# Feed-forward input products by one level of Strassen's scheme, gated features through DRAM, output projection as a stage of its own

## The chip, the core and the metric

The kernel runs on one core of a Trainium2 chip. The metric is device time in microseconds (us); the lower the better. Before the change three runs gave 3990.24, 3992.53 and 3998.9 us, median 3992.53.

## The reference, cut to what matters

Two trunk layers, each with a mixer and then a SwiGLU feed-forward block. There are 1152 tokens (128 of context, 1024 latent), the model width is 1024, the hidden width 2816. All data are float32. The change touches the feed-forward block of both layers alone:

```python
def swiglu(h, w_in, w_out):
    g, u = jnp.split(h @ w_in, 2, axis=-1)
    return (jax.nn.silu(g) * u) @ w_out
...
lat = lat + m_lat[5] * swiglu(modulate(rms_norm(lat, norm_ffn_g[layer]), m_lat[3], m_lat[4]), w_ffn_in[layer], w_ffn_out[layer])
```

## The kernel before

Activations are kept feature-major: 8 tiles of 128 features by 1152 tokens. Every float32 operand of a large product is split into a high part in the matmul's reduced float32 format (fp32r) and a low part, the rest; `mm3` (L79) then forms a product by three matmuls, high·high, high·low and low·high, into one PSUM bank. `hH`, `hL` are the two parts of the normed input, `wh`, `wl` those of a weight.

The feed-forward block (`ffn`, L1655) goes through 22 blocks `f` of 128 hidden features. For each it loads the gate and the up weights (8 DMAs of 128 KB), splits them (ScalarE copies to the high part at L73, VectorE subtracts at L74), and forms, for each of three groups of 384 tokens, the gate product and the up product: 3 x 2 x 8 x 3 = 144 matmuls of 384 columns. ScalarE applies silu (L1689), VectorE multiplies by the up product (L1690), ScalarE and GpSimd split the result into `gh`, `gl` (L1691, L1692). After each second `f` the output projection of the pair follows (`out_tg`, L760): 3 token groups x 8 output blocks x 6 matmuls, and VectorE adds the result to the residual `x` (L769). So a layer issues 22 x 144 = 3168 input matmuls and 1584 output matmuls, all of 384 columns.

Two other streams run beside it. At the block's start the norm of the last token group (`norm_fm`, L340) is still under way; `tail_step` advances it during `f` = 0. In layer 0 the modulation vector of layer 1 is formed on VectorE (`ada_vec`, L203: 96 steps, each a 256 KB load `aw` and two instructions over 512 elements at L221 or L223; the sums over partitions are 192 one-column matmuls, L229); `ffn` takes one or two steps after each token group.

The order on each engine's queue is set when the kernel is built, by a scheduler that follows the program's order and buffer releases; on the chip each queue runs in that order, except that semaphores make it wait. The lines around the change:

```python
hid.append((gh, gl))
if len(hid) == 2:
    ws = [self.out_w(wo, f - 1 + i, p) for i in range(2)]
    out = self.out_steps(l, 5, x, *zip(*hid), *zip(*ws), ps, post)
...
for _ in itertools.islice(side, 2 if (f + tg) % 2 else 1):
    pass
```

Of the kernel before, what the change touches and what calls it, by code (L numbers as in the profile page):

```python
# [20 lines left out]
P = 128  # L21
# [22 lines left out]
class Net:  # L44
# [25 lines left out]
    def split(self, hi, lo, src, scale=None):  # L70
        nc = self.nc
        if scale is None:
            nc.scalar.copy(hi, src)  # L73
            nc.vector.tensor_tensor(lo, src, hi, op=ALU.subtract)  # L74
        else:
            nc.scalar.mul(hi, src, scale)
            nc.vector.scalar_tensor_tensor(lo, src, scale, hi, op0=ALU.mult, op1=ALU.subtract)
# [1574 lines left out]
        return np_, hp, hH, hL  # L1652


    def ffn(self, l, x, hH, hL, p, ps, last, side):  # L1655
# [3 lines left out]
        hid = []  # L1659
        for f in range(NF):  # L1660
            WH, WL = [], []
            for kb in range(4):
                raw = self.t(p, [P, 2, 2, P], tag="wraw")
                for u in range(2):
                    nc.sync.dma_start(raw[:, :, u, :], wi[:, kb * 2 : kb * 2 + 2, u, f * P : (f + 1) * P])
                wh = self.t(p, [P, 2, 2, P], F32R, tag="wh")
                wl = self.t(p, [P, 2, 2, P], F32R, tag="wl")
                self.split(wh, wl, raw)
                WH.append(wh)
                WL.append(wl)  # L1670
# [3 lines left out]
            post = last() if f == NF - 1 else None  # L1674
            if len(hid) == 2:
                ws = [self.out_w(wo, f - 1 + i, p) for i in range(2)]
                out = self.out_steps(l, 5, x, *zip(*hid), *zip(*ws), ps, post)
            for tg in range(TG):
                sl = slice(tg * GW, (tg + 1) * GW)
                pg = []  # L1680
                for u in range(2):
                    pt = self.t(ps, [P, 512], tag="mm")
                    for k in range(KT):
                        self.mm3(pt[:, :GW], WH[k // 2][:, k % 2, u, :], WL[k // 2][:, k % 2, u, :], hH[k][:, sl], hL[k][:, sl], k == 0, k == KT - 1)
                    pg.append(pt)
                    if f == 0:
                        self.tail_step()
                s = self.t(p, [P, GW], tag="fs", bufs=2)
                nc.scalar.activation(s, pg[0][:, :GW], AF.Silu)  # L1689
                nc.vector.tensor_tensor(s, s, pg[1][:, :GW], op=ALU.mult)  # L1690
                nc.scalar.copy(gh[:, sl], s)  # L1691
                nc.gpsimd.tensor_tensor(gl[:, sl], s, gh[:, sl], op=ALU.subtract)  # L1692
                for _ in itertools.islice(side, 2 if (f + tg) % 2 else 1):
                    pass
                if post is not None:
                    for _ in range(KT):
                        next(out)
            if len(hid) == 2:
                for _ in out:
                    pass  # L1700
                hid = []


    def norm_out(self, x, gb, p, tg):
# [163 lines left out]
    def ffn_block(self, l, x, hp, hH, hL, np_):  # L1868

        nc = self.nc  # L1870
        with ExitStack() as es:
            p = _Bufs(es.enter_context(self.pool(f"ff{l}", "right" if l else "left")), {"wraw": 3, "wh": 6, "wl": 6, "gh": 3, "gl": 3, "owraw": 1, "owh": 2, "owl": 2, "aw": 2})
            ps = _Bufs(es.enter_context(self.pool(f"psf{l}", space=PSUM)), {"mm": 8})

            self.nps = ps

            def spill_norm(tg):
                sl = slice(tg * GW, (tg + 1) * GW)
                for k in range(KT):
                    nc.sync.dma_start(self.xsp[k, :, sl], x[k][:, sl])  # L1880
                yield from self.norm_fm(1, 1, 0, x, hH, hL, np_, tg)

            def last():
                if l == 0:
                    self.xsp = self.dram.tile([KT, P, TOK], F32, name="xsp")
                    return spill_norm
                np_.release()
                p2 = es.enter_context(self.pool("fin", "right"))
# [163 lines left out]
```

## Time and profile before

| | |
|---|---|
| runs | 3990.24, 3992.53, 3998.9 us |
| profiled execution | 3991.86 us, span 3990.1 us |
| mean granted TensorE clock | 0.973 of full speed |
| TensorE matmul busy | 3790.7 us of the span |
| VectorE, ScalarE, GpSimd busy | 2169.5, 1250.4, 711.9 us |
| feed-forward block, layer 0 | from 960.72 us to 1819.9 us |
| feed-forward block, layer 1 | from 3130.11 us to 3975.2 us |

PE is TensorE's matmul, PEld its weight load, DVE is VectorE, ACT ScalarE, POOL GpSimd, SP the queue that issues most DMAs. A duration is that of one instruction as the profiler saw it; matmuls overlap, so the time that one costs in a stream is the distance from start to start. PEclk is the granted clock.

### The profile page before, as it was taken

The numbers are of one execution on the slowest core, as the hardware profiler recorded it, in microseconds if no ns is written. First come the engines' busy times: TensorE is split into PE (matmuls) and PEld (weight loads), VectorE is DVE, ScalarE is ACT, GpSimd is POOL, SyncE is SP. The second block draws the span as 40 slices with busy tenths as digits, with TensorE's granted clock in tenths as the row PEclk, the third lists the DMA queues.
The fourth block names the chain that finished last, engine by engine and source line by source line (L and its number), as shares of the span: only waits on it lengthen the run. The fifth ranks groups of instructions, "written<-read, shape, count | busy, mean of one in ns | idle before, by whom it ended". The sixth has DMA issues, their size and how long they took to land.

```text
span 3990.1 us, 62872 instructions
## 1 busy us (share of the span) xinstructions
PE 3790.7 (95%) x23989; PEld 3559.6 (89%) x23989; DVE 2169.5 (54%) x5159; ACT 1250.4 (31%) x2930; POOL 711.9 (18%) x730
## 2 busy tenths in 40 slices
PE   8999997999999999998999998888888999999998
PEld 5899997999999999998989876776777999999998
DVE  5666665666454545345254656888875543343343
ACT  4555545555111111115232322233222411111112
POOL 3321202202100000012011232233322300000000
PEclk9999998999999999999999997999999999999999
DMA  6533316432222222213243434222223211111111
GB/s 203 150 105 91 95 52 163 126 85 88 67 80 64 85 64 80 69 46 116 87 129 102 163 123 142 66 70 63 64 64 103 64 38 45 41 37 43 43 40 53
DMA packets 378086, 339.98 MB, mean 85 GB/s; under 512 B 65428, under 2 KB 328720, under 8 KB 376248
## 3 DMA queue, kind: packets, MB, share of 16 engines
q1 hardware_dynamic: 359344, 324.37, 27.0%
q10 hardware_dynamic: 13160, 7.27, 0.7%
q0 software_dynamic: 5280, 4.31, 0.5%
q8 instruction: 190, 3.11, 0.3%
q14 instruction: 112, 0.92, 0.1%
HBM read 263.37 MB, written 72.38 MB: 84 GB/s over the span
## 4 chain that ended last, share of the span: by engine, by line
PE 78%; DVE 10%; DMA 5%; issue 3%; ACT 2%; POOL 1%; SPq 0%; ACTq 0%; DVEq 0%; POOLq 0%
PE mm L81 17%; PE mm L83 17%; PE mm L82 17%; PE o L522 3%; PE mm L390 2%; PE mm L392 2%; PE mm L391 2%; PE T L516 1%; DVE MB L1241 1%; DVE tf L1240 1%; PE mm L857 1%; PE A L1190 1%; PE mm L859 1%; PE mm L858 1%; PE S L558 1%
## 5 line engine op out<-in xcount | busy, mean ns | idle before, releaser
L81 PE MATMUL mm<-hH,wh 128*128 128x384 f32 x2544 | 865.1, 341 | 20.2 <-DVE nv L363 12.6
L82 PE MATMUL mm<-hL,wh 128*128 128x384 f32 x2544 | 860.6, 339 | 2.5 <-DVE hL L366 2.5
L83 PE MATMUL mm<-hH,wl 128*128 128x384 f32 x2544 | 859.8, 339 | 0.0
L769 DVE SCALAR_TENSOR_TENSOR x<-mm,mod,x 128x384 f32<-128x384 f32 (+2 forms) x896 | 431.5, 512 | 197.5 <-PE mm L83 195.8
L81 PEld LDWEIGHTS mm<-hH,wh 128*128 128x128 f32 x2544 | 480.0, 189 | 31.4 <-ACT wh L73 18.8
L82 PEld LDWEIGHTS mm<-hL,wh 128*128 128x128 f32 x2544 | 480.1, 189 | 5.6 <-DVE hL L366 2.7
L83 PEld LDWEIGHTS mm<-hH,wl 128*128 128x128 f32 x2544 | 480.0, 189 | 4.0 <-issue 2.9
L1692 POOL TENSOR_TENSOR gl<-fs,gh 128x384 fp32r<-128x384 f32 x132 | 140.4, 1063 | 1484.1 <-ACT gh L1691 1484.1
L74 DVE TENSOR_TENSOR wl<-wraw,wh 128x512 fp32r<-128x512 f32 (+2 forms) x360 | 217.9, 618 | 336.0 <-ACT wh L73 306.4
L82 PE MATMUL mm<-gl,owh 128*128 128x384 f32 x1056 | 353.0, 334 | 0.0
L83 PE MATMUL mm<-gh,owl 128*128 128x384 f32 x1056 | 352.9, 334 | 0.0
L81 PE MATMUL mm<-gh,owh 128*128 128x384 f32 x1056 | 350.4, 335 | 0.0
L1690 DVE TENSOR_TENSOR fs<-fs,mm 128x384 f32<-128x384 f32 x132 | 73.0, 553 | 430.3 <-PE mm L83 424.7
L73 ACT CAST wh<-wraw 128x512 fp32r<-128x512 f32 (+2 forms) x360 | 188.2, 530 | 205.5 <-DMA wraw<-in_w_ffn_in_dram 77.3
L73 ACT CAST owh<-owraw 128x1024 fp32r<-128x1024 f32 x60 | 62.9, 1049 | 489.7 <-PE mm L82 446.0
L390 PE MATMUL mm<-wh,hH 128*128 128x384 f32 x576 | 199.3, 346 | 3.8 <-ACT ist L408 3.7
L82 PEld LDWEIGHTS mm<-gl,owh 128*128 128x128 f32 x1056 | 198.3, 188 | 0.1
L83 PEld LDWEIGHTS mm<-gh,owl 128*128 128x128 f32 x1056 | 198.2, 188 | 0.0
L81 PEld LDWEIGHTS mm<-gh,owh 128*128 128x128 f32 x1056 | 197.8, 188 | 0.3 <-DVE x L769 0.3
L391 PE MATMUL mm<-wl,hH 128*128 128x384 f32 x576 | 195.3, 339 | 0.0
L392 PE MATMUL mm<-wh,hL 128*128 128x384 f32 x576 | 194.0, 338 | 0.0
L1689 ACT ACTIVATE fs<-mm 128x384 f32<-128x384 f32 x132 | 64.9, 492 | 383.5 <-PE mm L83 383.4
(385 smaller groups left out, 7437.8 us busy)
## 6 DMA issues: line engine op xcount, KB each, us to landing
wraw<-in_w_ffn_in_dram SPq DMA_DIRECT2D x352, 128.0 KB
aw<-in_w_ada_dram SPq DMA_DIRECT2D x160, 256.0 KB
owraw<-in_w_ffn_out_dram SPq DMA_DIRECT2D x44, 512.0 KB
F<-stg SPq DMA_DIRECT2D x34, 640.0 KB
stg<-st SPq DMA_DIRECT2D x12, 1536.0 KB
qkv<-ist SPq DMA_DIRECT2D x72, 192.0 KB
wraw<-in_w_in_attn_dram SPq DMA_DIRECT2D x64, 192.0 KB
nab<-rpbd SPq DMA_DIRECT2D x64, 192.0 KB
```

What stands on the lines that cost most here:

```text
L73: nc.scalar.copy(hi, src)
L74: nc.vector.tensor_tensor(lo, src, hi, op=ALU.subtract)
L81: mm(out, lhsT=wh, rhs=xh, start=first, stop=False)
L82: mm(out, lhsT=wh, rhs=xl, start=False, stop=False)
L83: mm(out, lhsT=wl, rhs=xh, start=False, stop=last)
L390: mm(pt[:, :ncol], lhsT=hH[k][:, c], rhs=WH[k], start=k == 0, stop=False)
L391: mm(pt[:, :ncol], lhsT=hH[k][:, c], rhs=WL[k], start=False, stop=False)
L392: mm(pt[:, :ncol], lhsT=hL[k][:, c], rhs=WH[k], start=False, stop=k == KT - 1)
L522: nc.tensor.matmul(o, lhsT=pT[:, i * P : (i + 1) * P], rhs=vs(b + i), start=b + i == 0, stop=b + i == nk - 1)
L769: self.nc.vector.scalar_tensor_tensor(x[f][:, c], pt[:, a:b], self.mod[l][jg][:, f, cd : cd + 1], x[f][:, c], op0=ALU.mult, op1=ALU.add)
L1690: nc.vector.tensor_tensor(s, s, pg[1][:, :GW], op=ALU.mult)
L1692: nc.gpsimd.tensor_tensor(gl[:, sl], s, gh[:, sl], op=ALU.subtract)
```

## The change

The input products of `f` = 1 to 21 use one level of Strassen's scheme in Winograd's form. The 2x2 blocks of the weights are (gate, up) by two halves of the 1024 input features, those of the activations the two halves of the features by two halves of the tokens (576 each). Seven block products take the place of eight: each has 2 column chunks of 288 x 4 feature tiles x 3 matmuls, so 168 matmuls of 288 columns for one `f`. `f` = 0 stays as it was.

The scheme needs combined operands. `forms` makes them from `hH` and `hL` at the start of each block: T1, T2, T3 in new tiles and a fourth in place of `hH[0:4]`, `hL[0:4]` in the second token half, in chunks of 192 and 384 columns, on VectorE, GpSimd and ScalarE; T2 is first read by the third product of `f` = 1, T3 by the fifth, the fourth form by the sixth. `prep` combines and splits the weights of each `f` (7 splits, 4 VectorE and 3 GpSimd subtractions of 512 elements, and 5 more additions or subtractions), two products ahead. PSUM results are copied and added by ScalarE and VectorE in pieces of 288 columns.

The gated features are stored to DRAM (`hdr`). The output projection (`ffn_out`) runs after all 22 `f`, over groups of 3, 4, 4, 4, 4 and 3 of them. It loads the features again per `f` and token group, and splits them on ScalarE and GpSimd; the weights come in halves, split by VectorE and GpSimd in turn. `ada_vec` now runs in this stage alone, 0.8 steps after each of the first 120 output blocks. Weights, features and `aw` share six buffers `raw`.

Diff, cut to its core:

```diff
+        def prep(f, i):
+
+            if i == 0:
+                W[f, 0] = split(R[f, 0, 0], nc.vector)
+            elif i == 1:
+                W[f, 1] = split(R[f, 1, 0], nc.gpsimd)
+            elif i == 2:
+                s1 = R[f, "s"] = self.t(p, [P, 512], tag="raw")
+                nc.gpsimd.tensor_tensor(s1, R[f, 0, 1], R[f, 1, 1], op=ALU.add)
+                nc.vector.tensor_tensor(R[f, 0, 1], R[f, 0, 0], R[f, 0, 1], op=ALU.subtract)
+                nc.vector.tensor_tensor(R[f, 0, 0], s1, R[f, 0, 0], op=ALU.subtract)
+                W[f, 2] = split(R[f, 0, 0], nc.vector)
+                nc.gpsimd.tensor_tensor(R[f, 1, 0], R[f, 1, 0], R[f, 0, 0], op=ALU.subtract)
+            else:
+                W[f, i] = split({3: R.get((f, "s")), 4: R[f, 0, 1], 5: R[f, 1, 1], 6: R[f, 1, 0]}[i], (nc.vector, nc.gpsimd)[i % 2])
...
+            for j, c in enumerate((n0, n1)):
+                pt = self.t(ps.pool, [P, 512], tag=bank) if new else bank[j]
+                for k in range(4):
+                    ks = slice(k * P, (k + 1) * P)
+                    xh, xl = op(k, c)
+                    o = pt[:, : HT // 2]
+                    mm(o, lhsT=wh[:, ks], rhs=xh, start=new and k == 0, stop=False, skip_group_check=True)
+                    mm(o, lhsT=wh[:, ks], rhs=xl, start=False, stop=False, skip_group_check=True)
+                    mm(o, lhsT=wl[:, ks], rhs=xh, start=False, stop=k == 3, skip_group_check=True)
...
-            gh = self.t(p, [P, TOK], F32R, tag="gh")
-            gl = self.t(p, [P, TOK], F32R, tag="gl")
-            hid.append((gh, gl))
...
+        for n, (f, i) in enumerate(seq):
+            if n + 2 < len(seq):
+                prep(*seq[n + 2])
+            for _ in itertools.islice(forms, 4):
+                pass
...
+        for k, c, d in units:
+            b = new(c)
+            e = new(c)
+            tt(V, b, hH[k][:, d], hH[k][:, c], S)
+            tt(G, e, hL[k][:, d], hL[k][:, c], S)
+            tt(V, b, b, e, A)
+            h, l = (o[:, k, c] for o in ops["T1"])
+            nc.scalar.copy(h, b)
+            tt(G, l, b, h, S)
+            g = new(c)
+            tt(V, g, hH[4 + k][:, d], b, S)
+            tt(V, g, g, hL[4 + k][:, d], A)
+            h, l = (o[:, k, c] for o in ops["T2"])
+            nc.scalar.copy(h, g)
+            tt(V, l, g, h, S)
+            yield
...
+        for n, (k, c, d) in enumerate(units):
+            b = new(c)
+            e = new(c)
+            tt(V, b, hH[4 + k][:, d], hH[k][:, d], S)
+            tt(G, e, hL[4 + k][:, d], hL[k][:, d], S)
+            tt(V, b, b, e, A)
+            h, l = (o[:, k, c] for o in ops["T3"])
+            nc.scalar.copy(h, b)
+            tt(G if n % 2 else V, l, b, h, S)
+            yield
...
+        def hidden(f, tg):
+            s = next(slots)
+            if s is None:
+                s = [self.t(p, [P, 512], F32R, tag=n)[:, :GW] for n in ("wh", "wl")]
+            w = self.t(p, [P, 512], tag="raw")[:, :GW]
+            nc.sync.dma_start(w, self.hdr[f][:, tg * GW : (tg + 1) * GW])
+            nc.scalar.copy(s[0], w)
+            nc.gpsimd.tensor_tensor(s[1], w, s[0], op=ALU.subtract)
+            return s
...
+            for _ in self.out_tg(l, 5, x, [a for a, _ in h], [b for _, b in h], WH, WL, ps, tg, post):
+                if todo:
+                    nxt.append(hidden(*todo.pop(0)))
+                elif ahead:
+                    weight(*ahead.pop(0))
+                due += 0.8
+                while due >= 1:
+                    due -= 1
+                    next(side, None)
```

VectorE's queue at the start of layer 0's block, before: weight splits (`wl`, `owl`) and the modulation sums (`aacc`).

```order
L74 TENSOR_TENSOR wl_11226<-wraw_11222,wh_11225 128x512
L74 TENSOR_TENSOR wl_11233<-wraw_11229,wh_11232 128x512
L221 TENSOR_SCALAR aacc_11363<-aw_11359,v_5_67 128x512 x2
L74 TENSOR_TENSOR wl_11240<-wraw_11236,wh_11239 128x512
L223 SCALAR_TENSOR_TENSOR aacc_11363<-aw_11361,v_5_67,aacc_11363 128x512 x2
```

The same queue some 70 instructions after the block's start now (T3 and T2 are the combined operands, `c` scratch, `B` a PSUM bank):

```order
L1827 TENSOR_TENSOR T3l_11252<-c_11604,T3h_11251 128x192
L1827 TENSOR_TENSOR c_11618<-hH_2652_10529,hH_2648_10525 128x192
L1827 TENSOR_TENSOR c_11611<-c_11611,c_11612 128x192
L1790 TENSOR_TENSOR c_11658<-c_11658,B_11696 128x288
L1827 TENSOR_TENSOR c_11625<-hH_2653_10530,hH_2649_10526 128x192
L1827 TENSOR_TENSOR c_11618<-c_11618,c_11619 128x192
L1827 TENSOR_TENSOR T3l_11252<-c_11618,T3h_11251 128x192
L1827 TENSOR_TENSOR c_11666<-hH_2650_10527,hH_2646_10523 128x384
L1677 TENSOR_TENSOR wl_11847<-raw_11581,wh_11846 128x512
```

The modulation sums have left this place; the combined operands, each read from SBUF twice, have come. GpSimd's queue at the same place, before (the norm's last `hL`, then the splits of gated features):

```order
L369 TENSOR_TENSOR hL_2660_10537<-nv_11344,hH_2652_10529 128x384
L369 TENSOR_TENSOR hL_2661_10538<-nv_11349,hH_2653_10530 128x384
L1692 TENSOR_TENSOR gl_11251<-fs_11479,gh_11250 128x384
L1692 TENSOR_TENSOR gl_11517<-fs_11580,gh_11516 128x384
L1692 TENSOR_TENSOR gl_11517<-fs_11643,gh_11516 128x384
```

and now:

```order
L1827 TENSOR_TENSOR c_11605<-hL_2658_10535,hL_2654_10531 128x192
L1827 TENSOR_TENSOR c_11612<-hL_2659_10536,hL_2655_10532 128x192
L1827 TENSOR_TENSOR c_11619<-hL_2660_10537,hL_2656_10533 128x192
L1677 TENSOR_TENSOR wl_11789<-raw_11585,wh_11788 128x512
L1827 TENSOR_TENSOR T3l_11252<-c_11611,T3h_11251 128x192
L1827 TENSOR_TENSOR c_11626<-hL_2661_10538,hL_2657_10534 128x192
L1718 TENSOR_TENSOR raw_11954<-raw_11886,raw_11888 128x512
```

So GpSimd's share of the combined operands stands in front of the weight splits that the next products need. VectorE's queue in the output stage of layer 0, where `hL_...` is now the place of an output weight's low part; before, one such stretch, in which residual additions (`x`) and modulation sums stand together:

```order
L221 TENSOR_SCALAR aacc_11723<-aw_11707,v_5_67 128x512 x2
L223 SCALAR_TENSOR_TENSOR aacc_11723<-aw_11721,v_5_67,aacc_11723 128x512 x2
L769 SCALAR_TENSOR_TENSOR x_1686_7094<-mm_11726,mod_17_105,x_1686_7094 128x128
L769 SCALAR_TENSOR_TENSOR x_1686_7094<-mm_11726,mod_17_105,x_1686_7094 128x256
L769 SCALAR_TENSOR_TENSOR x_1687_7095<-mm_11735,mod_17_105,x_1687_7095 128x128
```

and now:

```order
L224 SCALAR_TENSOR_TENSOR aacc_17634<-aw_17655,v_5_67,aacc_17634 128x512 x2
L770 SCALAR_TENSOR_TENSOR x_1689_7097<-mm_17703,mod_17_105,x_1689_7097 128x384
L1890 TENSOR_TENSOR hL_2660_10537<-raw_17735,hH_2652_10529 128x512
L224 SCALAR_TENSOR_TENSOR aacc_17634<-aw_17677,v_5_67,aacc_17634 128x512 x2
L770 SCALAR_TENSOR_TENSOR x_1690_7098<-mm_17721,mod_17_105,x_1690_7098 128x384
L224 SCALAR_TENSOR_TENSOR aacc_17634<-aw_17699,v_5_67,aacc_17634 128x512 x2
```

Two modulation sums now stand behind nearly each residual addition, through most of the stage.

## Rows read from the trace of the kernel before

**Rows 1.** The page's first two parts: busy time of each engine, and TensorE in 40 slices of the span with its granted clock.

```profile
PE 3790.7 (95%) x23989; PEld 3559.6 (89%) x23989; DVE 2169.5 (54%) x5159; ACT 1250.4 (31%) x2930; POOL 711.9 (18%) x730
...
PE   8999997999999999998999998888888999999998
...
PEclk9999998999999999999999997999999999999999
```

**Rows 2.** Busy time of the engines in the four stretches of the two feed-forward blocks, layer 0 and then layer 1, each cut where the first matmul of an output projection starts.

```profile
960.72:1023.06 62.34, 57.59 (x319) 56.98 (x320) 34.14 (x50) 26.11 (x46) 13.82 (x14) 0.92 0.38 116
1023.06:1819.90 796.84, 796.84 (x4671) 796.65 (x4671) 402.51 (x728) 151.74 (x272) 80.93 (x82) 1.00 0.24 71
3130.11:3185.88 55.77, 55.77 (x303) 55.73 (x304) 21.40 (x34) 26.47 (x49) 14.55 (x15) 0.94 0.28 85
3185.88:3975.20 789.32, 789.32 (x4513) 788.66 (x4513) 285.82 (x530) 139.51 (x249) 64.92 (x61) 1.00 0.14 41
```

**Rows 3.** TensorE in order of time inside layer 0's block, 384 columns: the first and the last of 57 matmuls, one row each (start, duration).

```profile
1749.77 0.33 PE L81 MATMUL mm<-hH,wh 128*128 128x384 f32 x1
...
1759.48 0.33 PE L83 MATMUL mm<-hH,wl 128*128 128x384 f32 x1
```

**Rows 4.** The same in the input projection of the recurrent mixer, 256 columns: the first and the last of 36.

```profile
1899.83 0.28 PE L859 MATMUL mm<-wh,hL 128*128 128x256 f32 x1
...
1903.99 0.28 PE L858 MATMUL mm<-wl,hH 128*128 128x256 f32 x1
```

**Rows 5.** Pieces of the chain that ended last, in order of time (start, length): two waits for a load, and sixteen one-column matmuls of the modulation.

```profile
964.93 4.61 DMA owraw<-in_w_ffn_out_dram
...
973.22 5.61 DMA aw<-in_w_ada_dram
...
1021.52 1.68 PE mm L229 x16
```

**Rows 6.** GpSimd by line and shape (times counted, busy us, mean ns of one, idle before).

```profile
L140 POOL TENSOR_TENSOR awl<-aw,awh 128x512 fp32r<-128x512 f32 x64 | 89.5, 1407 | 156.2 <-ACT awh L139 137.2 <-PE ada L147 18.8
...
L369 POOL TENSOR_TENSOR hL<-nv,hH 128x384 fp32r<-128x384 f32 x36 | 37.6, 1048 | 54.0 <-ACT nv L368 54.0
...
L369 POOL TENSOR_TENSOR hL<-nv,hH 128x256 fp32r<-128x256 f32 x18 | 13.9, 774 | 4.2 <-ACT nv L368 4.2
...
L369 POOL TENSOR_TENSOR hL<-nv,hH 128x128 fp32r<-128x128 f32 x18 | 8.9, 492 | 17.1 <-ACT nv L368 16.5 <-DVE hL L366 0.6
```

**Rows 7.** VectorE and ScalarE by line and shape.

```profile
L1690 DVE TENSOR_TENSOR fs<-fs,mm 128x384 f32<-128x384 f32 x132 | 73.0, 553 | 430.3 <-PE mm L83 424.7 <-ACT fs L1689 5.5
...
L73 ACT CAST wh<-wraw 128x512 fp32r<-128x512 f32 x176 | 109.3, 621 | 130.7 <-DMA wraw<-in_w_ffn_in_dram 77.3 <-PE mm L82 49.2 <-PE mm L83 3.3
...
L1689 ACT ACTIVATE fs<-mm 128x384 f32<-128x384 f32 x132 | 64.9, 492 | 383.5 <-PE mm L83 383.4
```

**Rows 8.** VectorE in order of time at the start of layer 0's block (start, duration); x2 and x4 are two or four instructions in one row.

```profile
951.87 0.99 DVE L366 SCALAR_TENSOR_TENSOR hL<-nv,mod,hH 128x384 fp32r<-128x384 f32 x1 [0.16 <-ACT hH L364]
...
953.31 0.60 DVE L363 SCALAR_TENSOR_TENSOR nv<-x,mod,mm 128x384 f32<-128x384 f32 x1
...
958.31 0.61 DVE L366 SCALAR_TENSOR_TENSOR hL<-nv,mod,hH 128x384 fp32r<-128x384 f32 x1
958.84 0.61 DVE L769 SCALAR_TENSOR_TENSOR x<-mm,mod,x 128x384 f32<-128x384 f32 x1
959.36 0.55 DVE L351 TENSOR_TENSOR nacc<-nacc,nsq 128x384 f32<-128x384 f32 x1
...
961.69 1.28 DVE L74 TENSOR_TENSOR wl<-wraw,wh 128x512 fp32r<-128x512 f32 x2
...
982.90 1.87 DVE L223 SCALAR_TENSOR_TENSOR aacc<-aw,v,aacc 128x512 f32<-128x512 f32 x2
...
985.96 1.40 DVE L223 SCALAR_TENSOR_TENSOR aacc<-aw,v,aacc 128x512 f32<-128x512 f32 x2
...
1026.75 1.38 DVE L769 SCALAR_TENSOR_TENSOR x<-mm,mod,x 128x128 f32<-128x128 f32 x4
```

**Rows 9.** GpSimd in order of time in the same stretch.

```profile
951.43 1.02 POOL L351 TENSOR_TENSOR nacc<-nacc,nsq 128x384 f32<-128x384 f32 x1 [0.34 <-ACT nsq L350]
953.10 1.02 POOL L369 TENSOR_TENSOR hL<-nv,hH 128x384 fp32r<-128x384 f32 x1 [0.65 <-ACT nv L368]
...
982.56 1.00 POOL L1692 TENSOR_TENSOR gl<-fs,gh 128x384 fp32r<-128x384 f32 x1 [17.18 <-ACT gh L1691]
```

**Rows 10.** From the list of waits (engine, line, waited for: us in total, times, longest).

```profile
DVE aacc L223 <- DMA aw<-in_w_ada_dram: 31.1, 29, 3.8
```

More of the change, by code (lines that the diff above doesn't have):

```diff
@@ L1652, in rec_out, with ffn @@
         return np_, hp, hH, hL
-    def ffn(self, l, x, hH, hL, p, ps, last, side):
+    def ffn(self, l, x, hH, hL, p, tp, cs, ps, side, last):
         nc, I = self.nc, self.I
         wi = I["w_ffn_in"][l].rearrange("(k p) (u f) -> p k u f", p=P, u=2)
-        wo = I["w_ffn_out"][l]
[L1659 to L1670, printed above, removed]
-            gh = self.t(p, [P, TOK], F32R, tag="gh")
-            gl = self.t(p, [P, TOK], F32R, tag="gl")
-            hid.append((gh, gl))
[L1674 to L1701, printed above, removed]
@@ new lines, in split @@
+        def split(w, eng):
+            wh = self.t(p, [P, 512], F32R, tag="wh")
+            wl = self.t(p, [P, 512], F32R, tag="wl")
+            nc.scalar.copy(wh, w)
+            eng.tensor_tensor(wl, w, wh, op=ALU.subtract)
+            return wh, wl
+        cw = {}
+        for u in range(2):
+            for a in range(2):
+                w, c = raw(0, a, u), slice((u * 2 + a) * 512, (u * 2 + a + 1) * 512)
+                cw[u, a] = T["T3h"][:, c], T["T3l"][:, c]
+                self.split(*cw[u, a], w)
@@ new lines, in ffn @@
+        forms = self.forms(hH, hL, ops, _Cycle(cs), p)
+        pg = []
+        for tg in range(TG):
+            sl = slice(tg * GW, (tg + 1) * GW)
+            for u in range(2):
+                pt = self.t(ps, [P, 512], tag="mm")
+                for k in range(KT):
+                    wh, wl = (w[:, (k % 4) * P : (k % 4 + 1) * P] for w in cw[u, k // 4])
+                    self.mm3(pt[:, :GW], wh, wl, hH[k][:, sl], hL[k][:, sl], k == 0, k == KT - 1)
+                pg.append(pt)
+                self.tail_step()
@@ new lines, in operand, with product @@
+        def operand(i):
+            if i in (2, 3, 4):
+                h, l_ = ops[("T2", "T1", "T3")[i - 2]]
+                return lambda k, c: (h[:, k, c], l_[:, k, c])
+            a, t = {0: (0, 0), 1: (1, 0), 5: (0, 1), 6: (1, 1)}[i]
+            return lambda k, c: tuple(q[a * 4 + k][:, t * HT + c.start : t * HT + c.stop] for q in (hH, hL))
+        def product(f, i, bank):
+            wh, wl = W.pop((f, i))
+            new, op = isinstance(bank, str), operand(i)
+            out = []
+            for j, c in enumerate((n0, n1)):
[7 more added lines that the diff above has]
+                    mm(o, lhsT=wl[:, ks], rhs=xh, start=False, stop=k == 3, skip_group_check=True)
+                out.append(pt)
+            return out
@@ L1891, in last @@
                 return lambda tg: self.norm_out(x, gb, p2, tg)
-            side = iter(()) if l else self.ada_vec(1, range(12), p)
-            self.ffn(l, x, hH, hL, p, ps, last, side)
+            side = iter(()) if l else self.ada_vec(1, range(12), _Alias(p, {"aw": "raw"}))
+            self.ffn(l, x, hH, hL, p, tp, cs, ps, side, last)
             if l:
```

156 lines of the change are left out of this document (151 added, 5 removed).

## The prediction

> **What bounds the kernel now.** I read the per-core view first: one core, granted clock 0.973, so no other core disturbs it. Then the page: TensorE is busy 95% of the span, VectorE 54%, ScalarE 31%, GpSimd 18%, and the slices show TensorE near full in nearly all of it [rows 1]. Then the stretches of the two feed-forward blocks [rows 2]: after the first 62.3 and 55.8 us TensorE is busy without a gap, at full clock, while VectorE works 402.5 of 796.8 us in layer 0 and 285.8 of 789.3 us in layer 1, and GpSimd a tenth. So in these blocks what counts is how many columns TensorE has to stream, and the others have room. The exception is the start of each block, where the granted clock is 0.92 and 0.94 and TensorE waits.
>
> What a matmul costs in the stream is its distance from the next: 57 matmuls of 384 columns start within 9.71 us, that is 9.71 / 56 = 0.1734 us each [rows 3]; 36 of 256 columns within 4.16 us, 4.16 / 35 = 0.1189 us [rows 4].
>
> With this the starts are priced. The first two `f` are 288 matmuls, 288 x 0.1734 = 49.9 us. Layer 0 takes 62.3 us, of which 1.7 us are modulation matmuls [rows 2, 5], so it loses 10.7 us; layer 1 loses 55.8 - 49.9 = 5.8 us.
>
> **Term 1, the products.** An `f` had 144 x 0.1734 = 24.97 us of TensorE. It now has 168 matmuls of 288 columns. The trace has no such width; between the two that it has, 0.1189 + 32 x (0.1734 - 0.1189) / 128 = 0.1325 us, or 22.26 us per `f`. (At 0.1189 us the `f` would be 19.97 us, at 0.1734 us it would be 29.13 us; the interpolation is trusted because both widths lie on one line through the stream's column rate, about 0.43 ns a column.) The gain is 2.71 us x 21 x 2 = 113.8 us. Seven eighths of the columns bring only 10.9%, as more and shorter matmuls each pay the fixed 12 to 13 ns again.
>
> The Trainium skill (TensorE: Matmul & The Clock Gate, section "Wait — 56ns, not 53.3ns?") gives N / 2.4 GHz plus about 2.5 ns from start to start. By it an `f` would go from 23.4 to 20.6 us and the gain would be 118 us. The rows here show 13 ns where it has 2.5, and they decide.
>
> Is TensorE fed at 22.3 us per `f`? Per `f`, ScalarE has 7 copies of 512 at 0.62 and 10 operations of 288 at about 0.4 (384 take 0.49) = 8.3 us; VectorE 6 operations of 512 at 0.64 and 12 of 288 at under 0.55 = 10 us; GpSimd 5 of 512 at 1.41 = 7 us [rows 6 to 8]. A weight is prepared two products (6.4 us) ahead and takes 0.62 + 1.41 us; an accumulator is copied within one product and a half (4.8 us), at about 0.8 us. The four stores of features per `f` stand in SP's queue ahead of weight loads and wait for their results, but each load is needed over 10 us later and takes about 5 [rows 5]. So I take 0; bounds -5 to +20 us (half a microsecond for each of 40 `f` when a wait in a queue is late).
>
> **Term 2, the start of each block.** The combined operands are made while `f` = 0 runs, and `f` = 1 waits for each. Per block, by the code: T1 and T2 take 5 VectorE and 2 GpSimd instructions for each of 8 pieces, T3 and the fourth form 2.5 and 1.5 each, half the pieces of 192 and half of 384 columns. With the rest of the norm and the weights of `f` = 0, 1 and part of 2, VectorE has 40 instructions of 192, 43 of 384 and 14 of 512 that read SBUF twice; GpSimd 20 of 192, 29 of 384 and 8 of 512.
>
> What decides is whether the two engines can work side by side. The rows say no. VectorE's `hL` of 384 takes 0.61 us at 958.31, with GpSimd idle, but 0.99 us at 951.87, where a GpSimd addition holds on until 951.43 + 1.02 = 952.45; it then ends 0.41 us later. An `aacc` pair takes 1.40 us, but 1.87 us at 982.90, beside GpSimd's 982.56 to 983.56. The `nv` at 953.31, which reads one operand from PSUM, takes 0.60 us in the middle of a GpSimd instruction [rows 8, 9]. So instructions that read SBUF twice on VectorE wait out GpSimd; and behind a waiting one stand, in the same queue, the weight splits and accumulator additions of the next products.
>
> Priced one after the other: GpSimd 20 x 0.63 (between 0.49 and 0.77) + 29 x 1.05 + 8 x 1.41 = 54.4 us [rows 6]; VectorE 0.41 us for 384 and in proportion, 40 x 0.21 + 43 x 0.41 + 14 x 0.55 = 33.7 us. Together 88 us from the block's start until the fourth form is complete, and about 4 us more for the product that reads it last and the next. By then TensorE has done `f` = 0 (24.97), `f` = 1 (22.26) and the first product of `f` = 2 (3.2) = 50.4 us of work in 92 us: it loses 41.6 us. Set against the 10.7 and 5.8 us lost now: 30.9 + 35.8 = +66.7 us for both layers. If the engines ran side by side, VectorE alone would need about 59 us (those 97 and some 18 others, at 0.38 for the shortest to 0.70 us) and the loss would be 13 us each, +9 us in all, or, if even that were hidden, -16.5 us; if a quarter of the time goes idle in the chains between the three engines, 22 us more each, +111 us. I take +67, since the rows show the exclusion itself and the queues are long enough to keep it filled. The granted clock is lower where TensorE waits (0.92 and 0.94 in these stretches now, 1.00 behind them [rows 2]); with more waits the products behind the last one may start at the lower level, 1.2 GHz, and I count one product at twice its time, 3 us a layer: +6 us.
>
> The Trainium skill (SBUF — State Buffer, section "Who interferes with whom") says that a VectorE instruction with two SBUF inputs and a GpSimd instruction that reads SBUF exclude each other for the whole instruction. Without that rule the sum of this change would be about -100 us, with it about -15 us; the rows above bear it out.
>
> **Term 3, the output stage of layer 0.** TensorE's output matmuls are as many as before. But VectorE now does all 192 modulation sums within its first 120 output blocks. TensorE needs there (24 x 9 + 96 x 12) x 0.1734 = 237.2 us, and 12 x 1.68 = 20.2 us for the modulation matmuls [rows 5]: 257 us. VectorE: 80 additions to `x` of 384 at 0.52 (start to start), 40 pairs of 128 and 256 at 0.69, 192 sums at 0.70, 19 weight halves at 0.64 = 216 us [rows 8]. GpSimd: 57 feature pieces at 1.05 and 19 weight halves at 1.41 = 87 us. Two thirds of VectorE's time (sums and weights, 147 of 216 us) reads SBUF twice and waits for GpSimd; a GpSimd instruction that meets an addition to `x` first costs half. That is about 0.8 x 87 = 69 us, so VectorE needs 285 us against 257. Behind a waiting sum in VectorE's queue stand the additions to `x` that free PSUM banks, so TensorE stops once its 8 banks are full. The banks take up some 6 us: +22 us. Bounds: 0 (216 us fits into 257) and 216 + 87 + the 31 us that the sums now wait for `aw` [rows 10] = 334, +77 us.
>
> Layer 1 has no modulation here: without the sums VectorE needs 216 - 134 = 82 us, and with all of GpSimd's 87 us on top it still fits behind TensorE; 0.
>
> **Term 4, from products to output.** The first weights and features of the output stage are loaded, through six buffers, during the last four products (12.7 us). Two rounds at 4.6 to 5.6 us a load [rows 5] and 2 us of splitting each take 13 to 15 us: +2 us a layer, +4; bounds 0 and +16.
>
> **Sum.** Made on the profiled execution, 3991.86 us (span 3990.1, 1.8 us around it; the median of three runs is 3992.53): 3991.9 - 113.8 + 67 + 6 + 22 + 4 = 3977 us.
>
> **Rivals.**
> 1. *VectorE and GpSimd disturb each other little* at the start, and the output stage fits: -113.8 + 9 + 4 = 3891 us, up to 3940 with half the price. For it: GpSimd is free 82% of the span, and pieces of 192 columns are short. Against it: the stretched instructions at 951.87 and 982.90.
> 2. *Slower:* VectorE becomes the bound of layer 0's output stage in full. All of GpSimd's time falls on it and the sums wait for loads through the six shared buffers: +77 in place of +22, so 4032 us. It decides the sign once that stage is over 37 us longer than 257 us. For it: the queue puts two sums behind nearly each addition, and `aw`, features and weights, about 186 loads in 257 us, need each buffer back after 8.3 us, when a load alone takes 4.6 to 5.6 us. Against it: VectorE's own time is 216 us.
> 3. *The products do not get cheaper:* a matmul of 288 columns costs as much as one of 384. Then an `f` takes 29.1 us, the products cost +175 us and the sum is about 4266 us. Against it the 256-column rows.
>
> **How the numbers follow.** Forecast 0.50, rival 1 0.22, rival 2 0.24, rival 3 0.02, anything else 0.02. The forecast's own range is 3950 to 4003. A difference under 0.2%, 8 us, can hardly be told from none. Six tenths of the forecast lie under 3984, some 0.16 between 3984 and 4000: faster 0.30 + 0.22 + 0.01 = 0.53, same 0.16, slower 0.04 + 0.24 + 0.02 + 0.01 = 0.31. The range leaves out the lower half of rival 1 and the upper half of rival 2: 3912 to 4030.
>
> **What will show it.** Matmuls of 288 columns should start every 0.132 us, and an `f` in mid-block take 22.3 us with TensorE full. In the first 90 to 95 us of each block TensorE should wait for VectorE and GpSimd at lines of `forms`, with VectorE's 384-column forms near 1 us where GpSimd works and 0.55 us where it doesn't. Layer 0's output stage should run longer than layer 1's by more than the 20 us of modulation matmuls, with VectorE without gaps. The prediction is wrong if the start takes under 70 or over 115 us, if mid-block `f` take over 22.8 us, or if layer 0's output stage keeps up with TensorE.

## The result, and the profile after

Four runs of the changed kernel gave a median of 3952.98 us (3946.16 to 3960.51), four of the kernel before 3991.39 us (3990.2 to 3998.9): ratio 0.990, 95% interval 0.9878 to 0.9922, so some 38 us or 1.0% faster. The profiled execution took 3954.28 us, its span 3952.3 us, 37.8 us less than before.

The page's first two parts, to be set beside [rows 1]:

```profile
PE 3709.5 (94%) x24997; PEld 3465.6 (88%) x24997; DVE 2362.6 (60%) x5461; ACT 1457.2 (37%) x3454; POOL 1128.2 (29%) x1064
...
PE   8999998999899999999999997888888989999998
...
PEclk9999998999899999999999997999998989999999
```

TensorE is busy 81 us less, but the span is only 38 us shorter: the rest has become time in which TensorE stands. Where it stands is told by six stretches, each layer's block cut where `f` = 4 starts and where the output stage starts. The columns are, as in [rows 2]: stretch, its length, busy time of TensorE, its weight loads, VectorE, ScalarE and GpSimd, granted clock, DMA share, GB/s.

```profile
956.33:1083.90 127.57, 108.79 (x663) 104.10 (x664) 98.46 (x154) 52.02 (x110) 70.71 (x66) 0.87 0.16 48
1083.90:1485.65 401.75, 401.75 (x3026) 401.75 (x3025) 177.10 (x323) 151.73 (x314) 125.42 (x96) 1.00 0.26 79
1485.65:1818.10 332.45, 316.71 (x1809) 313.60 (x1807) 270.87 (x463) 79.95 (x158) 114.54 (x101) 0.95 0.50 158
3127.98:3256.29 128.31, 108.72 (x664) 103.83 (x664) 96.40 (x156) 53.28 (x115) 71.18 (x68) 0.88 0.17 49
3256.29:3657.69 401.40, 401.40 (x3027) 401.40 (x3025) 176.50 (x323) 153.41 (x317) 125.87 (x97) 1.00 0.26 80
3657.69:3940.33 282.64, 282.64 (x1658) 282.24 (x1656) 121.11 (x241) 63.67 (x133) 85.94 (x80) 1.00 0.29 90
```

The middle stretches are 18 `f` each, without a gap and at full clock: 401.75 / 18 = 22.32 and 401.40 / 18 = 22.30 us per `f`. The starts hold 24.97 + 3 x 22.31 = 91.9 us of work in 127.6 and 128.3 us. The output stages issue the same matmuls, but layer 0's takes 49.8 us more.

By layer: layer 0's block took 859.2 us and now takes 861.8; layer 1's, to the start of its last output matmul, took 845.1 and now takes 809.4. Layer 0 gives its whole gain back; the kernel's gain is layer 1's.

TensorE in layer 0's mid-block, the first matmul of a product of 24 and the first of the next:

```profile
1300.74 0.30 PE L1745 MATMUL D<-hH,wh 128*128 128x288 f32 x1
...
1303.92 0.29 PE L1745 MATMUL E<-hH,wh 128*128 128x288 f32 x1
```

That is 3.18 / 24 = 0.1325 us a matmul of 288 columns. The columns that it replaced, in the kernel before: 271 matmuls of 384 columns in layer 1, and 144 in layer 0 (first and last of each).

```profile
1304.77 0.42 PE L81 MATMUL mm<-hH,wh 128*128 128x384 f32 x1
...
1329.64 0.33 PE L83 MATMUL mm<-hH,wl 128*128 128x384 f32 x1
...
3289.74 0.34 PE L83 MATMUL mm<-hH,wl 128*128 128x384 f32 x1
...
3337.44 0.34 PE L83 MATMUL mm<-hH,wl 128*128 128x384 f32 x1
```

In layer 0 24.87 / 143 = 0.1739 us each, in layer 1 47.70 / 270 = 0.1767: an `f` of layer 1 had cost 25.44 us, not 24.97.

**The start of a block.** TensorE at the start of layer 0's block, the waits that count (idle time and releaser in brackets):

```profile
995.76 0.40 PE L1745 MATMUL A<-hH,wh 128*128 128x288 f32 x1 [4.63 <-ACT c L1702]
...
1018.66 0.85 PE L1745 MATMUL A<-T3h,wh 128*128 128x288 f32 x2 [8.54 <-ACT T3h L1856]
1021.85 0.61 PE L1746 MATMUL A<-T3l,wh 128*128 128x288 f32 x1 [0.74 <-POOL T3l L1827]
...
1026.91 0.61 PE L1746 MATMUL A<-T3l,wh 128*128 128x288 f32 x1 [1.24 <-POOL T3l L1827]
...
1028.77 0.61 PE L1745 MATMUL A<-hH,wh 128*128 128x288 f32 x1 [0.53 <-ACT wh L1676]
```

TensorE is idle for 127.57 - 108.79 = 18.8 us of the stretch, and busy 16.9 us longer than its 91.9 us of work. Of these, 2.0 us are 15 small matmuls of the norm (L320, L336); the other 14.9 us are matmuls that take longer, because behind the waits they run at the lower level, 1.2 GHz: from 1030.62 to 1033.50 the granted clock is 0.50 and 12 steps take 0.24 us each, not 0.1325. Two fifths of the loss is the clock.

The last row is the first product of `f` = 2; it stands ahead of the sixth of `f` = 1, which needs the fourth form. VectorE and then GpSimd in the same place:

```profile
990.74 0.56 DVE L1827 TENSOR_TENSOR c<-hH,c 128x384 f32<-128x384 f32 x1
...
996.43 1.36 DVE L1827 TENSOR_TENSOR c<-hH,c 128x384 f32<-128x384 f32 x1
997.71 1.35 DVE L1827 TENSOR_TENSOR c<-hH 128x384 f32<-128x384 f32 x1
998.99 0.55 DVE L1827 TENSOR_TENSOR c<-c,hL 128x384 f32<-128x384 f32 x1
```

```profile
994.85 1.24 POOL L1827 TENSOR_TENSOR c<-hL 128x384 f32<-128x384 f32 x1 [1.43 <-DVE c L1827]
996.05 2.60 POOL L1827 TENSOR_TENSOR T1l<-c,T1h 128x384 fp32r<-128x384 f32 x2
...
1043.77 1.02 POOL L1827 TENSOR_TENSOR hL<-c,hH 128x384 fp32r<-128x384 f32 x1 [1.65 <-ACT hH L1865]
```

The same subtraction takes VectorE 0.56 us alone and 1.36 us behind GpSimd. The last combined operand is done at 1044.79, 88.5 us after the block's start.

**Layer 0's output stage.** The list of TensorE's waits in it (total, times, longest), and VectorE's modulation sums by shape (busy, mean ns of one):

```profile
PE mm L230 <- DVE aacc L224: 12.1, 7, 2.8
PE mm L82 <- ACT wh L74: 2.8, 1, 2.8
PE mm L82 <- DVE c L1814: 0.7, 1, 0.7
```

```profile
L224 DVE SCALAR_TENSOR_TENSOR aacc<-aw,v,aacc 128x512 f32<-128x512 f32 x168 | 148.7, 920 | 0.0
```

TensorE waits for the most part (12.1 of 15.7 us) where it meets the one-column matmuls of the modulation (L230) before VectorE has the last sum; a sum takes 920 ns, where two took 1.40 us [rows 8]. The wait of 2.8 us for ScalarE ends the stage: it is for a weight of the next mixer. Another 316.7 - 294.9 = 21.8 us is TensorE's busy time over its own matmuls (294.9 is 1584 x 0.1734 + 20.2 of modulation). By the distances from start to start, 14.5 us of it are 384-column matmuls that take longer, most of them behind these waits at half clock, some 4.5 us one-column matmuls that take longer, and 2.8 us 30 small matmuls of the next norm, which this stage already held in the kernel before.

### The profile page after: what moved, and what is told of

It is laid out like the page before. It is cut to its first block, busy times and chain, and to the rows that moved or that the text cites. A ratio compares the mean times of both kernels' runs of the same rounds, so it can differ in the third digit from the quotient of the medians.

```text
span 3952.3 us, 67315 instructions
## 1 busy us (share of the span) xinstructions
PE 3709.5 (94%) x24997; PEld 3465.6 (88%) x24997; DVE 2362.6 (60%) x5461; ACT 1457.2 (37%) x3454; POOL 1128.2 (29%) x1064
## 4 chain that ended last, share of the span: by engine, by line
PE 54%; DVE 12%; DMA 5%; issue 2%; POOL 1%; ACT 1%; SPq 0%; DVEq 0%; ACTq 0%; POOLq 0%
PE mm L82 6%; PE mm L84 6%; PE mm L83 6%; PE A L1745 3%; PE A L1747 3%; PE A L1746 3%; PE E L1747 2%; PE E L1745 2%; PE E L1746 2%; DVE c L1827 1%; PE mm L858 1%; DVE MB L1242 1%; PE mm L860 1%; PE mm L859 1%; PE A L1191 1%
## 5 line engine op out<-in xcount | busy, mean ns | idle before, releaser
L770 DVE SCALAR_TENSOR_TENSOR x<-mm,mod,x 128x128 f32<-128x128 f32 (+1 forms) x576 | 278.9, 511 | 213.5 <-PE mm L84 212.3
L1677 POOL TENSOR_TENSOR wl<-raw,wh 128x512 fp32r<-128x512 f32 x126 | 172.1, 1366 | 588.3 <-ACT wh L1676 584.0
L1676 ACT CAST wh<-raw 128x512 fp32r<-128x512 f32 x294 | 182.2, 620 | 346.6 <-PE A L1746 123.1
L82 PE MATMUL mm<-hH,wh 128*128 128x384 f32 x432 | 152.5, 354 | 2.8 <-ACT wh L74 2.8
L84 PE MATMUL mm<-hH,wl 128*128 128x384 f32 x432 | 148.7, 346 | 2.9 <-DVE rst L908 2.4
L224 DVE SCALAR_TENSOR_TENSOR aacc<-aw,v,aacc 128x512 f32<-128x512 f32 x168 | 148.7, 920 | 0.0
L82 PE MATMUL mm<-mh,owh 128*128 128x384 f32 x384 | 141.1, 382 | 7.6 <-ACT mh L74 5.3
L83 PE MATMUL mm<-hL,wh 128*128 128x384 f32 x432 | 148.1, 344 | 0.0
L84 PE MATMUL mm<-mh,owl 128*128 128x384 f32 x384 | 133.5, 348 | 2.0 <-DVE owl L75 2.0
L83 PE MATMUL mm<-ml,owh 128*128 128x384 f32 x384 | 135.4, 353 | 0.0
L1790 DVE TENSOR_TENSOR c<-c,B 128x288 f32<-128x288 f32 x84 | 38.1, 454 | 153.5 <-PE B L1747 83.4
```

What stands on the lines that cost most here:

```text
L82: mm(out, lhsT=wh, rhs=xh, start=first, stop=False)
L83: mm(out, lhsT=wh, rhs=xl, start=False, stop=False)
L84: mm(out, lhsT=wl, rhs=xh, start=False, stop=last)
L770: self.nc.vector.scalar_tensor_tensor(x[f][:, c], pt[:, a:b], self.mod[l][jg][:, f, cd : cd + 1], x[f][:, c], op0=ALU.mult, op1=ALU.add)
L1677: eng.tensor_tensor(wl, w, wh, op=ALU.subtract)
```

## Experiments

Stretches are given as: start to `f` = 4, in layer 0 and 1 (127.6 and 128.3 in the changed kernel); layer 0's output stage (332.5); and between the blocks, from there to layer 1's first block matmul (1309.9). Layer 1's output stage was 282.6 us in all.

**Combined operands on VectorE alone**

```diff
-        tt, V, G = ..., nc.vector, nc.gpsimd
+        tt, V, G = ..., nc.vector, nc.vector
```

> The changed kernel, with every instruction of the combined operands that GpSimd did given to VectorE (40 a block: 20 of 192 and 20 of 384 columns). Theory (VectorE and GpSimd exclude each other on SBUF, so the start of a block lasts as long as the two together): GpSimd gives up 20 x 0.65 + 20 x 1.1 = 35 us of the 88.5 us in which the combined operands were made, VectorE takes on 20 x 0.27 + 20 x 0.47 = 15 us, so they are complete some 68 us after the block's start instead of 88.5; the stretch from the block's start to f = 4 goes from 127.6 and 128.3 us to about 112 in each layer (work 91.9), and the time from 3953 to about 3922 us. Rival (side by side, VectorE's own queue is what is late): VectorE has 15 us more, the stretch grows by about 10 us a layer, about 3973 us.

Measured: 3952.36 us, ratio 0.9899 (0.9886 to 0.9912). The stretches are 127.1 and 125.1: the theory's 112 is missed, the rival's +10 too. In layer 0 the combined operands were complete 86.0 us after the block's start, not after 68, with VectorE busy for 71.8 of them; so by itself this run does not bear the theory out. GpSimd in layer 0's start shows a part of the reason, and TensorE's wait behind it:

```profile
994.69 3.70 POOL L1677 TENSOR_TENSOR wl<-raw,wh 128x512 fp32r<-128x512 f32 x1 [9.46 <-ACT wh L1676]
...
1024.78 5.81 POOL L1677 TENSOR_TENSOR wl<-raw,wh 128x512 fp32r<-128x512 f32 x1 [18.88 <-DVE hL L1827]
```

```profile
1030.64 0.61 PE L1747 MATMUL B<-hH,wl 128*128 128x288 f32 x1 [4.26 <-POOL wl L1677]
```

VectorE at the end of each of these two splits:

```profile
997.18 0.44 DVE L1790 TENSOR_TENSOR c<-c,B 128x288 f32<-128x288 f32 x1
997.54 1.06 DVE L1827 TENSOR_TENSOR c<-hL,hL 128x192 f32<-128x192 f32 x1
...
1028.91 0.55 DVE L1827 TENSOR_TENSOR c<-hL,T2l 128x384 f32<-128x384 f32 x1
1029.38 0.44 DVE L1804 TENSOR_TENSOR c<-c,E 128x288 f32<-128x288 f32 x1
```

A GpSimd split of 1.3 to 1.4 us took 5.81 and ended at 1030.59. VectorE ran combined operands without a pause until 1029.38; there it came to an addition that reads one operand from PSUM (`c<-c,E`, L1804, 0.44 us), and then it paused. The split of 3.70 us ended the same way, 1.2 us after VectorE had begun such an addition at 997.18 (`c<-c,B`, L1790), though VectorE did not pause there. So the exclusion works the other way as well, and weight splits had become late. That called for the next one.

**The weights of `f` = 1 and 2 on VectorE too**

```diff
+            gp = nc.vector if f <= 2 else nc.gpsimd
-                W[f, 1] = split(R[f, 1, 0], nc.gpsimd)
+                W[f, 1] = split(R[f, 1, 0], gp)
```

(likewise the other three places of `prep` with `nc.gpsimd`)

> The combined operands on VectorE alone, as in the first experiment, and the five GpSimd instructions of the weights of f = 1 and f = 2 on VectorE too (10 a block, 6 us on VectorE). Theory (a GpSimd split starves while VectorE runs without a gap: one took 5.81 us, TensorE waited 4.3 and 1.7 us for two of them, at half clock behind that): these waits go, and the stretch from the block's start to f = 4 falls from 127.1 and 125.1 us to about 118 in each layer; 3952 to about 3937 us. Rival (VectorE's own work sets the start): 6 us more on VectorE, the stretch grows to 130 to 133 us, about 3964.

Measured: 3934.78 us, 0.9859 (0.9838 to 0.9881); 116.9 and 119.7. As the theory said. VectorE does more and the start is 8.6 to 10.7 us shorter, so in the changed kernel it was not VectorE's own work that was late. In layer 0 the combined operands are now complete after 76.0 us, VectorE busy for 71.0 of them: here its own work is the limit. That GpSimd is the slower engine for the same instruction would also shorten the start when it is relieved; that the two hold each other up is shown by the stretched instructions, and this run can't tell the two shares apart. (An `f`'s weights take GpSimd five instructions, three splits and two of the additions and subtractions; of the latter `prep` makes four besides the splits, not five as the section on the change has it.)

**Low parts of the output stage on VectorE**

```diff
-            (nc.gpsimd if half else nc.vector).tensor_tensor(wl, w, wh, op=ALU.subtract)
+            nc.vector.tensor_tensor(wl, w, wh, op=ALU.subtract)
-            nc.gpsimd.tensor_tensor(s[1], w, s[0], op=ALU.subtract)
+            nc.vector.tensor_tensor(s[1], w, s[0], op=ALU.subtract)
```

> The changed kernel, with all low parts of the output stage (features and weights) on VectorE instead of GpSimd. Theory A (VectorE loses to GpSimd: the sums take 0.92 us instead of 0.70 because they wait out 87 us of GpSimd): VectorE needs 216 + 57 x 0.47 + 19 x 0.6 = 254 us in the first 120 output blocks without being held up, the sums go back to 0.70 to 0.75 us, layer 0's output stage from 332 to about 305 us, the time from 3953 to about 3926. Theory B (VectorE is blocked because the low part of a weight stands in its queue and waits for a late load, 27 us in this stage): now 57 + 19 more instructions on VectorE wait for loads, the stage grows by 10 to 40 us, 3963 to 3993. Layer 1's output stage stays at 282.6 us by both.

Measured: 3928.64 us, 0.9845 (0.9831 to 0.9859); layer 0's output stage 313.2 us. The stage and the sums:

```profile
1485.23:1798.43 313.20, 306.40 (x1808) 303.76 (x1806) 270.85 (x534) 76.18 (x151) 14.68 (x19) 0.98 0.54 164
```

```profile
L224 DVE SCALAR_TENSOR_TENSOR aacc<-aw,v,aacc 128x512 f32<-128x512 f32 x167 | 119.3, 743 | 0.0
```

VectorE's busy time is 270.85 us with 534 instructions, and it was 270.87 with 463: the 71 more cost nothing, because part of what the page called busy had been waiting for GpSimd (a sum falls from 920 to 743 ns). Theory A; B's growth did not come.

**All low parts of the output weights on GpSimd**

```diff
-            (nc.gpsimd if half else nc.vector).tensor_tensor(wl, w, wh, op=ALU.subtract)
+            nc.gpsimd.tensor_tensor(wl, w, wh, op=ALU.subtract)
```

> The changed kernel, with all low parts of the output weights on GpSimd (the half that VectorE did as well). Theory A (exclusion is the price): GpSimd has 22 x 1.4 = 31 us more, of which VectorE waits out most, and 15 us less of its own; layer 0's output stage grows by about 10 us to 342, 3963 us. Theory B (VectorE is blocked by weights whose load is late): the 27 us that VectorE waits there go, the stage falls from 332 to about 312 us, 3933 us.

Measured: 3955.44 us, 0.9906 (0.9891 to 0.9921); output stage 340.1 us, as theory A said (the total by itself can't be told from the changed kernel's), with sums at 980 ns:

```profile
L224 DVE SCALAR_TENSOR_TENSOR aacc<-aw,v,aacc 128x512 f32<-128x512 f32 x168 | 159.8, 980 | 29.4 <-DMA aw<-in_w_ada_dram 29.2
```

**The one-column matmuls two blocks behind the last sum**

```diff
-                p2 = self.t(self.nps, [P, 512], tag="mm")
+                yield; yield; p2 = self.t(self.nps, [P, 512], tag="mm")
...
-                due += 0.8
+                due += 1.0
```

> The changed kernel, with the modulation sums of a column group made at one step an output block instead of 0.8, and its one-column matmuls two blocks (4.2 us) behind the last sum in the program. Theory C (only the place is wrong: TensorE arrives at the one-column matmuls 0.3 to 2.8 us before the last sum is done, 12 us in all, and each stop lowers the granted clock afterwards, some 16 us): both go, layer 0's output stage falls from 332 to about 305 us, about 3926 us. Rival (VectorE is short of time over the whole stage): sums that come faster are late all the same, the waits grow or move to the residual additions, 332 us or more, 3953 or more.

Measured: 3943.94 us, 0.988 (0.9867 to 0.9893); output stage 325.9 us, sums still 909 ns. Neither: the place accounts for some 6.5 us, not for 27. Of the 12.1 us that TensorE waited for the sums 8.4 are left, in later places, so VectorE is short of time, as the rival has it, if not by all of the 332 us.

**`f` = 1 plain as well**

```diff
+        for u in range(2):
+            for a in range(2):
+                cw[u, a] = split(r1[a, u], nc.vector)
+            for tg in range(TG):
+                plain(u, tg)
...
-        seq = [(f, i) for f in range(1, NF) for i in range(7)]
+        seq = [(f, i) for f in range(2, NF) for i in range(7)]
```

> The changed kernel with f = 1 computed like f = 0, by 144 plain matmuls of 384 columns; the combined operands stay on both engines, and T3 is first read in f = 2. It computes the same. Theory (the start costs what TensorE lacks in work until the combined operands are complete, 88.5 us after the block's start): TensorE has 2 x 24.97 us of plain matmuls and 32 us of products of f = 2 and 3 that need no late operand, so of the 35.7 us lost in each layer some 12 are left (the norm's 3, some half clock, a few us at T3); the plain f = 1 costs 2.66 us more. f = 4 starts 106 to 108 us after the block instead of 127.6 and 128.3; 3953 to about 3912 us. Rival (the loss comes from queues on ScalarE, VectorE and GpSimd, wherever the combined operands are needed): 25 us or more stay lost, f = 4 starts after 120 us or more, 3940 to 3955.

Measured: 3893.24 us, 0.9765 (0.9742 to 0.9788), but the stretches are 114.3 and 117.9, longer than 106 to 108. TensorE is idle for 10.1 and 10.8 us of them, 4.2 and 3.8 of these in waits for GpSimd's splits and for the fourth form, so part of the rival holds. The total is better than the stretches allow: between the blocks it took 1273.8 us. (Layer 1's block starts at 3077.73 in this kernel. The 1275.7 and 34 us of an expectation below were counted to 3079.56, a few matmuls into the block; its 518 us should be 519.) This stretch in that kernel, and in the changed one:

```profile
1803.90:3077.73 1273.83, 1191.92 (x8469) 1033.84 (x8469) 825.61 (x2320) 401.19 (x933) 329.93 (x343) 0.96 0.32 99
```

```profile
1818.10:3127.98 1309.88, 1194.45 (x8470) 1031.05 (x8470) 833.08 (x2320) 402.12 (x933) 330.09 (x343) 0.96 0.32 97
```

The work is the same, TensorE's idle time falls from 115.4 to 81.9 us. No line of these stages was edited, but the scheduler, which orders the queues when the kernel is built, gave TensorE and VectorE another order in the recurrent mixer.

**`f` = 1 plain, and the output stage's low parts on VectorE** (both diffs above)

> f = 1 plain (combined operands on both engines) and the low parts of the output stage on VectorE. The two stages between the feed-forward blocks have here the instruction order of the changed kernel, row for row on TensorE; the kernel with f = 1 plain alone had another order there, on TensorE and VectorE, and was 34 us shorter between the blocks, although no line of those stages was edited. If the order made these 34 us: between the blocks 1310 us again (1275.7 there), products stages 516 and 518 us as in that kernel, layer 0's output stage 313 us, sum 3953 - 13 - 12 - 19 = about 3909 us, slower than without the second edit (3893). If the 34 us were a gain of the plain f = 1 itself or of the chip's state, they are here too: about 3875 us.

Measured: 3908.97 us, 0.9795 (0.9779 to 0.981); between the blocks 1309.1 us, output stage 309.2, starts 113.9 and 117.1. With nearly the old order of the mixer (8320 of 8469 TensorE matmuls stand in the same place as in the changed kernel, 6069 in the kernel before this one) these 36 us are gone, as the first reading said. They are no gain of the plain `f` = 1. They go with that order; the kernel of the weights' move, measured on the same chip as the one with `f` = 1 plain alone, took 1309.0 us there, so the chip was not the reason.

**All helpful edits, with and without the weights**

```diff
+            gp = nc.vector if f <= 3 else nc.gpsimd
```

This line, with `f` = 1 plain, the combined operands on VectorE and the output stage's low parts on VectorE:

> The changed kernel with the helpful edits together: f = 1 plain, the combined operands and the weights of f = 2 and 3 on VectorE, and all low parts of the output stage on VectorE. If the effects add: f = 4 starts some 105 us after each block's start (-22 us a layer), layer 0's output stage takes 313 us (-19): about 3885 to 3890 us. If GpSimd's absence only moves the queue to VectorE in the start, the start is no better than with GpSimd: 3890 to 3900.

Measured: 3871.35 us, 0.9705 (0.9682 to 0.9727); starts 102.3 and 102.4 against 94.6 of work, output stage 307.9, between the blocks 1303.0, with yet another order there. All three are shorter than the added effects (105, 313, 1310), hence 14 us less than expected, some 7 of them from between the blocks. It beats the changed kernel by some 2% and the one before by 3.0%. The same without this line (the 504 and 497 us in its expectation are 504.1 and 503.8: layer 1's block of the kernel above starts at 3073.42, and the 497 was counted from a matmul inside it):

> f = 1 plain, the combined operands on VectorE, the weights left as in the changed kernel, the low parts of the output stage on VectorE. Theory (GpSimd starves beside a VectorE that never pauses, so its weight splits must leave it too): the products stages lie between the 516 and 518 us of f = 1 plain alone and the 504 and 497 us with the weights of f = 2 and 3 on VectorE, near 510. Rival (the splits don't matter once f = 1 is plain): 504 and 497 us. Layer 0's output stage 308 to 313 us. Between the blocks the order differs from all kernels so far: 1275 to 1310 us. Total 3850 to 3890 us.

Measured: 3882.22 us, 0.9726 (0.9709 to 0.9744); starts 105.4 and 107.8, the stretch from the block's start to the output stage 507.2 and 509.3 us, where it is 504.1 and 503.8 with the line and 516.2 and 519.3 with `f` = 1 plain alone. As the theory said, by a smaller margin: two of GpSimd's splits took 5.18 and 6.09 us beside a busy VectorE. The intervals of the two totals overlap; the 3.1 and 5.5 us are read from the stretches. Then all helpful edits together with the delayed one-column matmuls:

> All helpful edits (f = 1 plain, combined operands and the weights of f = 2 and 3 on VectorE, low parts of the output stage on VectorE) and the one-column matmuls two blocks behind the last sum. Theory (with VectorE no longer held up, what is left in layer 0's output stage is mostly the places where TensorE meets the last sum): 307.9 us fall to about 300, 275 of output matmuls and 20 of modulation matmuls; 3871 to 3863 us if the stages between the blocks stay at 1310. Rival: what is left there is loads and the end of the block; 308 us stay.

Measured: 3868.69 us, 0.9705 (0.9688 to 0.9722), with an output stage of 310.2 us. The rival: once VectorE is free of GpSimd, the place of these matmuls is worth nothing. (Between the blocks this kernel took 1294.5 us, 8 less than the one without the delay, in another order.)

## Why the prediction was right, and where its terms were off

The forecast was 3977 us for the profiled execution, which took 3954.3; faster was the likelier side, and 3950 to 4003 the forecast's own range. Its structure held (a gain in the products, mostly eaten up at the starts and in layer 0's output stage), with sizes off both ways. That the time fell inside the range is in part luck: terms 1 and 2 came out 25.6 us better than forecast, layer 0's output stage 10.6 us worse.

| term | forecast | measured | worked out as |
|---|---|---|---|
| 1, products | -113.8 | -122.0 | 21 x (24.99 - 22.32) + 21 x (25.44 - 22.30) |
| 2, starts, with the clock | +67 + 6 | +55.6 | (35.7 - 10.7) + (36.4 - 5.8) |
| 3 and 4, layer 0's output stage and its handover | +22 + 2 | +34.6 | 332.45 - 274.7 - 20.2 - 3.0 |
| 3 and 4, layer 1 | 0 + 2 | 0 | 282.6 less 274.7 and 72 transposes |
| rest | 0 | -5.8 | what is left of 37.6 us |

The 24.99 us are 144 times 0.1736, the mean distance of the 2880 input matmuls in the second stretch of [rows 2]. The 3.0 us are the next norm's small matmuls, which the block of before held as well. Of the rest, 4.4 us is layer 0's block starting earlier; the kernels of this study, with the stages ahead of it unedited, started it at 949.6 to 960.8 us. The other 1.4 us are within the rounding of the unit costs.

**Term 1.** "0.1325 us, or 22.26 us per `f`" measured 0.1325 and 22.3: the straight line between two widths carries, and rival 3 is out. No stall showed in mid-block, as taken. What failed is the step "57 matmuls of 384 columns start within 9.71 us, that is 9.71 / 56 = 0.1734 us each": those 57 are of layer 0, and it was used for both layers. The trace of before had 0.1767 for layer 1, worth 9.9 us over 21 `f`. Why the same matmul was 1.9% slower there is open. It is no matter of the clock or of the stretch: the output matmuls that stand between these products in layer 1 took 0.1735. The prediction's "fixed 12 to 13 ns" is what is left over the columns at 2.4 GHz; by its own 0.43 ns a column some 10 ns are left. Neither enters its sum. The Trainium skill's 2.5 ns on top of N / 2.4 GHz (TensorE: Matmul & The Clock Gate, "Wait — 56ns, not 53.3ns?") doesn't agree: 288 columns are 120 ns at 2.4 GHz and 122.5 ns by it, and 132.5 were measured, so 12.5 ns on top.

**Term 2.** That the two engines exclude each other is shown by the stretched instructions, and the weights' move to VectorE agrees; "together 88 us from the block's start until the fourth form is complete" measured 88.5. Two steps were off. "By then TensorE has done `f` = 0, `f` = 1 and the first product of `f` = 2": the scheduler had put more of `f` = 2 ahead of the late products of `f` = 1, so TensorE had other work. And "I count one product at twice its time, 3 us a layer" for the clock was far too little: half clock cost 14.9 us of layer 0's 35.7. The idle time was less than forecast (18.8 us, where 41.6 were taken), the clock took part of it back: 35.7 and 36.4 us lost instead of 44.6. Rival 1 (little disturbance, 13 us a layer) is out. The SBUF rule that the prediction took from the Trainium skill (SBUF — State Buffer, "Who interferes with whom") agrees with 1.36 against 0.56 us.

**Term 3.** VectorE was late, because of GpSimd: 19 us of the 34.6 go when GpSimd leaves the stage, and 7.6 us come when it does more. But "TensorE stops once its 8 banks are full" was the wrong place. It stopped at the modulation's own one-column matmuls, whose place in its queue the scheduler had fixed, and "VectorE without gaps" did not show: it was busy 270.9 of 332.5 us. The size was off for the clock again: some 19 us of matmuls that took longer, which the working did not count. Rival 2 was to decide the sign once the stage was 37 us longer, and it was 34.6, close to that mark; with the larger term 1 and the smaller starts that were measured, some 70 us would have been needed.

**Term 4** was 0.7 us in layer 0 and nothing in layer 1, in place of 2 each: the loads were early enough.

## What to carry to other kernels

Price a wait of TensorE at about twice its idle time when the matmuls behind it run at the lower clock, as they did here (18.8 us idle and 14.9 us of slower matmuls in one stretch, 15.7 and some 19 in another), and take the unit cost of a matmul from each stretch that it is used for. When VectorE is the helper that is late, look at what GpSimd does beside it: instructions that read SBUF twice on both engines add up one after the other, and here the slower engine's share was worth moving to the faster one, weight splits included. Compare kernels stretch by stretch, from the first matmul of each: a build-time scheduler can reorder a stage that nobody edited.

## What was not expected of the hardware

- GpSimd can starve beside VectorE instructions that read SBUF twice and follow each other without a pause: a split of 1.3 to 1.4 us took 5.81 us. It went through, as one of 3.70 us did, when VectorE came to an instruction with an operand in PSUM, in the second case without a pause. It is no rule, though: in the changed kernel GpSimd got in behind a single VectorE instruction (1.24 us at 994.85), and what decides who is next is open. VectorE behind GpSimd lost less than one GpSimd instruction (1.36 us in place of 0.56; the longest combined operand at the start of a block took 1.64).
- A helper's busy time can stay the same when it gets 71 more instructions to do (270.87 and 270.85 us): the profile counts waiting for the other engine as busy.
- The same 384-column matmul of an input product took 0.1734 to 0.1739 us in layer 0 and 0.1767 us in layer 1, at full granted clock and without gaps, and in the changed kernel's `f` = 0 again 0.1741 and 0.1766; the output matmuls of layer 1 took 0.1735.
